# Weight splits queued before the last recurrence and its scans, and odd Fourier weights cast among the evictions of the even map

## The chip, the cores and the metric

The kernel runs on one core of a Trainium2 chip. The metric is the device time of one execution in microseconds (us), the median over runs. Lower is better.

## What is computed

One layer of a diffusion backbone for 512 latent tokens and 256 context tokens of width 1024, all in float32. The first half is a token mixer, the second a layer of sixteen experts.

```python
h = modulate(rmsnorm(x), shift, scale)              # latent and context alike
z = h @ w_in                                        # [Fourier | RG-LRU input | GeLU gate | gate A | gate B]
y_four = fourier_mix(z_F) @ w_four                  # real part of a 2-D DFT, 4 groups of 128 channels
u = dwconv(z_X); r = rglru_bidir(u)                 # gates, exp, linear scans in both directions
y_rnn = (gelu(z_G) * r) @ w_lru
x = x + g1 * ((sigmoid(z_A) * y_four + sigmoid(z_B) * y_rnn) @ w_out)
x = x + g2 * expert_choice_ffn(modulate(rmsnorm(x), ...))   # 16 experts: gate, up, down
out = rmsnorm(x)
```

## The kernel before, in words

Everything is written out by hand: each engine runs its instructions in the order of the Python code, and an instruction that waits holds up all that stands behind it on its engine.

**Weights and splits.** A product with float32 accuracy is made of three TensorE passes (`mm3`, L428 to L430): high part by high part, high by low, low by high. So each block of weights (1024 rows by 256 columns, `raw`, 1 MB) is split after it has landed: ScalarE casts the high part `wH` (L230), and VectorE subtracts it from the block to make the low part `wL` (L231), each in two halves. `split(j)` does this for block j, `use(j)` splits block j+1 and hands out block j, `SP.pop(j)` hands out block j alone. There are two buffers of `wH` and `wL`, so block j+2 is split into the buffers of block j, and its cast waits until TensorE has read block j for the last time. There are three buffers of `raw`. The list `seq` gives the order of the loads on SyncE's queue, and each split or accumulation that frees a buffer issues the next (`load_next`). The blocks of `w_ada` (for the modulation vectors) stand between them at places given by `ada_at`: VectorE accumulates such a block in nine instructions (`ada_acc`, L273 to L278), and TensorE reduces it over the partitions later (`ada_red`, L289 or L293).

**The Fourier stage** (some 55 to 95 us). For each of eight column blocks j TensorE computes the even part `ye` (weights `we`, the sum `wo` of two halves of `w_four`; L430, L642), and afterwards for each j the odd part `yo` (weights `wd4`, split from the difference `A4` by `split_four`, L609 and L610). `ye` is copied by ScalarE into a tile `y4[j]` (L643). There are four PSUM buffers for `ye` and `yo`. Behind each copy stands `modulate`, which prepares one block of the context (`cH` on ScalarE L422, GpSimd L423, `cL` on VectorE L426). The difference A4 - B4 is made by GpSimd in four instructions (L541), behind a chain of small ones for the recurrence (`lru_b`). The tiles `y4` lie in a pool that is opened where the pool `ad` was closed, and B4 had its place in that pool.

**The recurrence** (95 to 260 us). For each of eight heads h: `zX` (TensorE), convolution (VectorE), gates, `lru(h-1)` (ScalarE tanh, exp, sqrt; VectorE L701, L711; GpSimd L712) and `scans(h-2)` (VectorE L720 to L724, GpSimd L726, which adds the two directions into `yr`).

**The GeLU stage** (245 to 307 us). Blocks J_G to J_G+3 give `zG(0)` to `zG(3)`, 48 matmuls each, then follows `zB`. The loop over i writes out, for each engine, the products of block i, and behind them: for i = 0 `scans(6)` and `lru(7)`; for i = 1 `scans(7)`, the close of the recurrence's pools, the opening of the pool for `gH` and `gL`, and `g_evac(0)`; for i = 2 and 3 `g_evac(i - 1)`, and at last `g_evac(3)`. `g_evac(i)` does for two heads a GeLU on ScalarE (L791), the product with `yr` on VectorE (L792), the cast to `gH` (L793) and the subtraction to `gL` (L794). In i = 3 a tick after the fifth k of `zG(3)` calls `ada_red`.

**The rest.** Gate B and the map `w_lru` (`zB`, `yR`), the output projection, the router, and from about 465 us on the experts. Their 302 MB of weights are loaded through a ring of buffers (`eload`): the first loads are issued in the output projection, and each further one when TensorE has used a tile of the ring.

Of the kernel before, what the change touches and what calls it, by code (L numbers as in the profile page):

```python
# [12 lines left out]
AF = mybir.ActivationFunctionType  # L13
# [63 lines left out]
def layer(ctx: ExitStack, tc: tile.TileContext, I, out):  # L77
    nc = tc.nc
    pe, act, dve, pool = nc.tensor, nc.scalar, nc.vector, nc.gpsimd
# [78 lines left out]
    for i in range(4):  # L158
# [3 lines left out]
    J_X, J_G, J_B, J_O = 2, 10, 14, 22  # L162
# [1 line left out]
    ada_cols = ([1024 + 256 * i for i in range(4)] + [256 * i for i in range(4)] +  # L164
                [2048 + 256 * i for i in range(4)] + [4096 + 256 * i for i in range(4)] +
                [3072 + 256 * i for i in range(4)] + [5120 + 256 * i for i in range(4)])
    ada_at = {j: [p] for j, p in zip([J_X + 1, J_X + 3, J_X + 5, J_X + 7, J_G + 1] + list(range(J_G + 3, J_O + 2)), range(8, 24))}
    seq = [("a", 0), ("a", 4), ("f", 0), ("a", 1), ("f", 1), ("a", 5), ("f", 2), ("a", 2), ("a", 6), ("f", 3), ("a", 3), ("a", 7)]
    seq += [("4", 0), ("4", 1), ("w", 2)]
    for i in range(2, NW):  # L170
# [9 lines left out]
    def load_next():  # L180
        n = st["load"]
        if n >= len(seq):
            return
        st["load"] += 1
        kind, j = seq[n]
        if n in (3, 4, 8, 9, 13):
            t = ad.tile([P, 8, 256], F32, tag="ad", bufs=2, name=f"raw{n}")
        else:
            t = stage.tile([P, 8, 256], F32, tag="raw", bufs=AHEAD, name=f"raw{n}")
        if kind == "w":  # L190
            nc.sync.dma_start(t, W[j][0])
        elif kind == "f":
            t = f2(t)[:, 0:1024].rearrange("p (k e) -> p k e", k=2)
            nc.sync.dma_start(t, w_in[256 * j:256 * j + 256, 0:512].rearrange("(k p) e -> p k e", p=P))
        elif kind == "4":
            t = t.rearrange("p (a k) e -> p a (k e)", a=2)
            if j:
                nc.sync.dma_start(t, I["w4b"])
            else:
                for c in range(2):  # L200
                    nc.sync.dma_start(t[64 * c:64 * c + 64], flat(I["w_four"], P * c * D, [[D, 64], [256 * D, 2], [1, D]]))
        else:
            nc.sync.dma_start(t, w_ada[:, ada_cols[j]:ada_cols[j] + 256].rearrange("(p k) e -> p k e", k=KD))
        raws[kind, j] = t
        if n == 11:
            nc.sync.dma_start(dc, I["dft_c"])
            nc.sync.dma_start(xc, I["ctx"][0].rearrange("(n p) d -> p n d", p=P))
        if n == 13:
            nc.sync.dma_start(dt, I["dft_t"])
            for q in range(4):  # L210
                nc.sync.dma_start(w6[32 * q:32 * q + 4, :].rearrange("p (a e) -> p a e", a=2),
                                  flat(I["w_four"], 64 * D + P * q, [[P * D, 4], [512, 2], [1, P]]))
# [6 lines left out]
    SP = {}  # L219

    def split_half(j, h, copy=None):
        if j >= NW:
            return
        nk = W[j][1]
        if j not in SP:
            SP[j] = (take("w", j), stage.tile([P, nk, 256], F32R, tag="wH", bufs=2, name=f"wH{j}"),
                     stage.tile([P, nk, 256], F32R, tag="wL", bufs=2, name=f"wL{j}"))
        raw, wH, wL = SP[j]
        a = slice(h * nk // 2, (h + 1) * nk // 2)
        (copy or act.copy)(wH[:, a], raw[:, a])  # L230
        dve.tensor_sub(wL[:, a], raw[:, a], wH[:, a].bitcast(F32))  # L231
        if h:
            SP[j] = (wH, wL)
            load_next()

    def split(j, copy=None):
        for h in range(2):
            split_half(j, h, copy)
# [182 lines left out]
    def modulate(k, v, src, tmp, dH, dL, eng, late=()):  # L421
        act.activation(dH, src, AF.Identity, bias=modc[:, k, v:v + 1], scale=s1[:, k, v:v + 1])  # L422
        eng.tensor_scalar(tmp, src, s1[:, k, v:v + 1], modc[:, k, v:v + 1], op0=OP.mult, op1=OP.add)  # L423
        while late:
            late.pop()()
        dve.tensor_sub(dL, tmp, dH.bitcast(F32))  # L426
# [94 lines left out]
    A4, B4 = take("4", 0), take("4", 1)  # L521
# [29 lines left out]
    def use(j, copy=None):  # L551
        split(j + 1, copy)
        return SP.pop(j)
# [50 lines left out]
    def split_four(t, a, o):  # L604
        if not o:
            o.append(stage.tile([P, 2, D], F32R, tag="wH", bufs=2, name="w4H"))
            o.append(stage.tile([P, 2, D], F32R, tag="wL", bufs=2, name="w4L"))
        q = slice(512 * a, 512 * a + 512)
        act.copy(o[0][:, :, q], t[:, :, q])  # L609
        dve.tensor_sub(o[1][:, :, q], t[:, :, q], o[0][:, :, q].bitcast(F32))  # L610
# [3 lines left out]
    we, wd4 = [], []  # L614
# [8 lines left out]
    z = ct(0, "f6")  # L623
    cosines(z[:, 0:258], lambda b: P6[:, b].rearrange("p q c -> p (q c)"), E6.rearrange("p q c -> p (q c)"))
    put((8, 9), z[:, 0:258])
    for a in range(2):
        split_four(A4, a, wd4)
    load_next()

    def y4_mm(o, w, f, j, last):  # L630
        cc = slice(P * j, P * j + P)
# [4 lines left out]
    for j in range(KD):  # L636
        z = ct(1 + j, "ye")[:, 0:258]
        y4_mm(z, we, 0, j, False)
        q, c6 = 32 * (j % 4), P * (j // 4)
        r6 = slice(q, q + 32)  # L640
        for i, (a, b) in enumerate(((0, 8), (0, 9), (1, 8))):
            pe.matmul(z, w6s[r6, a, c6:c6 + P], fT[r6, b, 0:258], start=False, stop=i == 2, tile_position=(q, 0))  # L642
        act.copy(y4[j][:, 0:257], z[:, 0:257])  # L643
        modulate(j, 1, xcT[:, j, :], xcT[:, j, :], cH[:, j, :], cL[:, j, :], pool)
    split_half(J_X, 0)
    for j in range(KD):
        z = ct(1 + j, "yo")[:, 0:256]
# [12 lines left out]
    yr = bt.tile([P, H, T], F32, tag="bt", name="yr")  # L660
# [32 lines left out]
    def lru(h, mid=None):  # L693
        u = U.pop(h)
        r = {(d, i): GP.pop((h, d, i)) for d in range(2) for i in range(2)}
        tps = {}
        for d in range(2):
            q = 8 * d + h
            tps[d] = lr.tile([P, TA], F32, tag="tp", bufs=3, name=f"tp{h}")
            act.activation(tps[d], r[d, 0], AF.Tanh, bias=c2[:, q:q + 1], scale=c2[:, q:q + 1])  # L700
            dve.scalar_tensor_tensor(r[d, 1], r[d, 1], 1.0, u, op0=OP.add, op1=OP.mult)  # L701
        for d in range(2):
            q = 8 * d + h
            act.activation(r[d, 0], r[d, 0], AF.Exp, bias=c4n[:, q:q + 1], scale=c4n[:, q:q + 1])
        for d in range(2):
            act.activation(tps[d], tps[d], AF.Sqrt, scale=0.25)
        if mid:
            mid()
        for d in range(2):
            a, b, s = r[d, 0], r[d, 1], tps[d]  # L710
            dve.scalar_tensor_tensor(s, a, 1.0, s, op0=OP.add, op1=OP.mult)  # L711
            pool.tensor_tensor(b, s, b, op=OP.mult)  # L712
        LR[h] = r, tps

    def scans(h):
        r, tps = LR.pop(h)
        for d in range(2):
            a, b, s = r[d, 0], r[d, 1], tps[d]
            if d == 0:
                dve.tensor_tensor_scan(s, a, b, 0.0, OP.mult, OP.add)  # L720
            else:
                dve.tensor_tensor_scan(s[:, 0:TC][:, ::-1], a[:, 0:TC][:, ::-1], b[:, 0:TC][:, ::-1],
                                       0.0, OP.mult, OP.add)
                dve.tensor_tensor_scan(s[:, TC:TA][:, ::-1], a[:, TC:TA][:, ::-1], b[:, TC:TA][:, ::-1],  # L724
                                       s[:, 0:1], OP.mult, OP.add)
        pool.tensor_tensor(yr[:, h, :], tps[0][:, TC:TA], tps[1][:, TC:TA], op=OP.add)  # L726
# [57 lines left out]

    zG = {}

    def g_evac(i):
        z = zG.pop(i)
        for c in range(2):
            j = 2 * i + c  # L790
            act.activation(z[:, c, :], z[:, c, :], AF.Gelu_apprx_tanh)  # L791
            dve.tensor_mul(yr[:, j, :], z[:, c, :], yr[:, j, :])  # L792
            act.copy(gH[:, j, :], yr[:, j, :])  # L793
            dve.tensor_sub(gL[:, j, :], yr[:, j, :], gH[:, j, :].bitcast(F32))  # L794

# [9 lines left out]

    TICK = {0: g_tick, 3: ada_tick}
    for i in range(4):
        w = use(J_G + i) if i else SP.pop(J_G)
        zG[i] = (gt if i == 2 else zt)("zG")
        for c in range(2):  # L810
            zcols(w, zG[i][:, c, :], c, lambda k: TICK.get(i, lambda k: None)(KD * c + k))
        if i == 0:
            scans(H - 2)
            lru(H - 1)
            continue
        if i == 1:
            scans(H - 1)
            close_lr()
            close_hc()
            gp, close_gp = sb("gp", "right")  # L820
            gH = gp.tile([P, H, T], F32R, name="gH")
            gL = gp.tile([P, H, T], F32R, name="gL")
        g_evac(i - 1)
        if i == 1:
            ada_red()
            ada_acc(J_G + 1)
    g_evac(3)

    mH = []
# [2 lines left out]
    for i in range(4):  # L832
        w = use(J_B + 2 * i)
        th = sg.tile([P, 2, 512], F32, tag="th", bufs=2, name="thB")
        for c in range(2):
            z = ct(c, "zB")
# [123 lines left out]
    w = use(J_O)  # L960
# [420 lines left out]
```

## Time and profile before

| | |
|---|---|
| median of 3 runs | 1184.53 us (1184.46 to 1188.39) |
| the profiled execution's own time | 1183.71 us |
| its span, first to last instruction | 1181.9 us |
| busy in the span: TensorE, VectorE, ScalarE, GpSimd | 96%, 47%, 25%, 10% |
| mean granted TensorE clock | 0.989 |
| read from HBM | 364.43 MB |

The profile shows one execution, with times in us from the start of its span. The busy share is an average over stages with different limits: where an engine waits, and for whom, is read stage by stage. A granted clock of 1.00 is 2.4 GHz, 0.50 is 1.2 GHz.

### The profile page before, as it was taken

How to read it: one execution, taken by the hardware profiler on the slowest of the kernel's cores; microseconds unless marked ns; L12 is line 12 of the kernel's file. 1: busy time of each engine (PE TensorE's matmuls, PEld its weight loads, DVE VectorE, ACT ScalarE, POOL GpSimd, SP SyncE). 2: the span in 40 equal slices, each digit the busy share in tenths (PEclk: the TensorE clock that was granted, in tenths of full speed). 3: DMA queues.
4: the chain of work that ended last, by engine and by line, in shares of the span. 5: the costliest groups of instructions: out<-in, count | busy, mean ns of one | idle time of the engine just before them, and what ended most of it. 6: DMA issues, size and time to landing. Idle time of an engine off the chain costs nothing. (4 is left out here: it accounts for less than half of the span.)

```text
span 1181.9 us, 16740 instructions
## 1 busy us (share of the span) xinstructions
PE 1140.5 (96%) x6870; PEld 684.7 (58%) x6888; DVE 552.3 (47%) x1090; ACT 294.1 (25%) x457; POOL 115.0 (10%) x120
## 2 busy tenths in 40 slices
PE   8999999998999999999999999999999999999986
PEld 4778777776888897545445445454444345345333
DVE  5545898877767675233432332342332332332124
ACT  5452776764423222101001001001001001001004
POOL 4163333422000000000000000000000000000002
PEclk9989999998999999999999999999999999999998
DMA  8922321332544697889999999999999999999995
GB/s 303 320 88 92 125 80 54 116 107 67 194 167 150 206 367 318 311 348 416 367 424 424 424 423 424 423 424 423 424 423 424 425 423 424 423 425 424 424 413 217
DMA packets 115435, 368.01 MB, mean 311 GB/s; under 512 B 8912, under 2 KB 61656, under 8 KB 115232
## 3 DMA queue, kind: packets, MB, share of 16 engines
q1 hardware_dynamic: 112688, 363.52, 77.6%
q0 software_dynamic: 1088, 2.18, 0.6%
q10 hardware_dynamic: 1584, 1.25, 0.4%
q8 instruction: 54, 0.88, 0.3%
q14 instruction: 21, 0.17, 0.0%
HBM read 364.43 MB, written 2.10 MB: 310 GB/s over the span
## 5 line engine op out<-in xcount | busy, mean ns | idle before, releaser
L1152 PE MATMUL G<-ew,g 128*64 128x384 f32 x960 | 171.4, 493 | 2.6 <-DMA ew<-in_w_gate_e 2.1
L1152 PE MATMUL U<-ew,g 128*64 128x384 f32 x928 | 166.0, 493 | 6.8 <-DMA ew<-in_w_up_e 6.7
L1177 DVE TENSOR_TENSOR ac<-ac,sc 128x512 f32<-128x512 f32 x112 | 72.0, 684 | 97.5 <-PE sc L1171 97.5
L1152 PEld LDWEIGHTS G<-ew,g 128*64 128x64 f32 x960 | 62.9, 136 | 85.0 <-issue 64.0
L1152 PEld LDWEIGHTS U<-ew,g 128*64 128x64 f32 x928 | 60.7, 136 | 86.9 <-issue 59.8
L1288 POOL TENSOR_TENSOR o<-ac,ew 128x512 f32<-128x512 f32 (+1 forms) x8 | 7.8, 1000 | 880.7 <-ACT o L1284 880.7
L1254 DVE SCALAR_TENSOR_TENSOR wc<-Y,gc,g 128x512 f32<-128x512 f32 x15 | 11.3, 751 | 146.2 <-PE Y L1251 146.2
L1251 PE MATMUL Y<-ew,wa 128*64 128x512 f32 x312 | 74.1, 597 | 2.2 <-ACT wa L1240 2.2
L1251 PE MATMUL Y<-ew,wd 128*64 128x512 f32 x312 | 74.9, 594 | 0.0
L231 DVE TENSOR_TENSOR wL<-raw,wH 128x1024 fp32r<-128x1024 f32 x48 | 64.7, 1382 | 14.9 <-ACT wH L230 14.8
L1240 ACT COPY wa<-T 128x384 f32<-128x384 f32 x16 | 7.7, 479 | 250.3 <-PE T L1239 250.3
L1213 ACT ACTIVATE wc<-G 128x768 f32<-128x768 f32 x16 | 13.0, 811 | 180.5 <-PE G L1152 180.5
L230 ACT CAST wH<-raw 128x1024 fp32r<-128x1024 f32 x48 | 48.2, 1044 | 22.0 <-PE zO L430 18.5
L1124 PEld LDWEIGHTS xg<-wa,x 128*128 128x128 f32 x448 | 51.1, 192 | 0.2
L1124 PE MATMUL xg<-wa,x 128*128 128x128 f32 x448 | 51.2, 275 | 0.0
L1251 PEld LDWEIGHTS Y<-ew,wd 128*64 128x64 f32 x312 | 23.5, 137 | 47.3 <-issue 39.6
L1090 DVE TENSOR_SCALAR wc<-wa,score 128x128 bf16<-128x128 f32 (+3 forms) x63 | 24.0, 380 | 56.3 <-ACT wa L1083 56.3
L1257 ACT CAST wb<-wc 128x512 fp32r<-128x512 f32 x15 | 9.3, 618 | 153.8 <-DVE wc L1254 153.8
L1251 PEld LDWEIGHTS Y<-ew,wa 128*64 128x64 f32 x312 | 21.4, 136 | 43.7 <-issue 35.4
L712 POOL TENSOR_TENSOR th<-tp,th 128x768 f32<-128x768 f32 x16 | 38.5, 2426 | 63.1 <-DVE tp L711 63.1
L1171 PEld LDWEIGHTS sc<-wb 64*128 64x128 f32 x240 | 23.6, 184 | 35.9 <-issue 35.9
L688 ACT ACTIVATE th<-ga,lru_c 128x768 f32<-128x768 f32 x32 | 28.9, 905 | 41.8 <-PE ga L686 41.8
(361 smaller groups left out, 2181.5 us busy)
## 6 DMA issues: line engine op xcount, KB each, us to landing
ew<-in_w_gate_e SPq DMA_DIRECT2D x120, 768.0 KB, 14.7
ew<-in_w_up_e SPq DMA_DIRECT2D x116, 768.0 KB, 14.7
ew<-in_w_down_e SPq DMA_DIRECT2D x111, 768.0 KB, 14.7
raw<-in_w_ada SPq DMA_DIRECT2D x24, 1024.0 KB, 5.5
raw<-in_w_in SPq DMA_DIRECT2D x16, 1024.0 KB, 5.1
wd<-in_w_down_e SPq DMA_DIRECT2D x8, 768.0 KB, 12.0
we<-in_w_down_e SPq DMA_DIRECT2D x8, 768.0 KB, 14.8
raw<-in_w_lru SPq DMA_DIRECT2D x4, 1024.0 KB
```

What stands on the lines that cost most here:

```text
L230: (copy or act.copy)(wH[:, a], raw[:, a])
L231: dve.tensor_sub(wL[:, a], raw[:, a], wH[:, a].bitcast(F32))
L688: act.activation(t, gf[:, 256:1024], AF.Tanh, bias=(hbi if i else hba)[:, 8 * d + h:8 * d + h + 1], scale=0.5)
L712: pool.tensor_tensor(b, s, b, op=OP.mult)
L1090: dve.tensor_scalar(GT[c][:, 0:m], sB[:, 0:m], s, None, op0=OP.is_lt)
L1124: pe.matmul(a[k // 4][:, P * (k % 4) + q.start:P * (k % 4) + q.stop], x[:, n, P * k:P * k + P], oh[:, n, q], start=n == 0, stop=n == NT - 1)
L1152: pe.matmul(t[64 * f:64 * f + 64, n, 0:384], xg[:, k, c:c + CAP], w[:, o:o + 384], start=k == 0, stop=k == KD - 1, tile_position=(0, 64 * f))
L1171: pe.matmul(a[dh][:, c], w, v, start=j == 0, stop=j == 1, tile_position=(64 * dh, 0))
L1177: dve.tensor_add(xs, xs if e else x[:, n, q], a[dh])
L1213: act.activation(v3(sl), G[:, :, 0:384], AF.Silu)
L1251: pe.matmul(yp[64 * dh:64 * dh + 64, :], hT[j // 3][:, j % 3, 64 * f:64 * f + 64], w[:, 512 * i:512 * i + 512], start=f == 0 and j == 0, s ...
L1254: dve.scalar_tensor_tensor(y, yp, gc[:, e % 3:e % 3 + 1], g2, op0=OP.mult, op1=OP.mult)
```

## The change

Three things are moved, nothing is added or left out in the computation.

1. In the Fourier stage the two halves of `split_four(A4, ...)` no longer stand ahead of the copies of `ye`, but behind the copy and the `modulate` of j = 4 and of j = 6. The load behind them moves to the end of that loop.
2. In the GeLU stage the split of J_G+2 stands between `scans(6)` and `lru(7)`, and the split of J_G+3 ahead of `scans(7)`. Blocks J_G+1 and J_G+2 are therefore handed out without a further split. Before, J_G+2 was split behind `lru(7)`, and J_G+3 behind `g_evac(0)` and an accumulation.
3. The GeLU and the product of heads 0 and 1 (`g_mul`) stand ahead of the split of J_G+3; `g_evac(0)` has only the cast and the subtraction left. The block of `w_ada` that was loaded ahead of J_G+3 is now loaded behind it (`ada_at`), and still accumulated at the end of i = 1.

```diff
-    ada_at = {j: [p] for j, p in zip([J_X + 1, J_X + 3, J_X + 5, J_X + 7, J_G + 1] + list(range(J_G + 3, J_O + 2)), range(8, 24))}
+    ada_at = {j: [p] for j, p in zip([J_X + 1, J_X + 3, J_X + 5, J_X + 7, J_G + 2] + list(range(J_G + 3, J_O + 2)), range(8, 24))}
...
     put((8, 9), z[:, 0:258])
-    for a in range(2):
-        split_four(A4, a, wd4)
-    load_next()
...
         act.copy(y4[j][:, 0:257], z[:, 0:257])
         modulate(j, 1, xcT[:, j, :], xcT[:, j, :], cH[:, j, :], cL[:, j, :], pool)
+        if j in (4, 6):
+            split_four(A4, j // 2 - 2, wd4)
+    load_next()
     split_half(J_X, 0)
...
+    def g_mul(i, c):
+        j = 2 * i + c
+        z = zG[i]
+        act.activation(z[:, c, :], z[:, c, :], AF.Gelu_apprx_tanh)
+        dve.tensor_mul(yr[:, j, :], z[:, c, :], yr[:, j, :])
+
     def g_evac(i):
-        z = zG.pop(i)
         for c in range(2):
             j = 2 * i + c
-            act.activation(z[:, c, :], z[:, c, :], AF.Gelu_apprx_tanh)
-            dve.tensor_mul(yr[:, j, :], z[:, c, :], yr[:, j, :])
+            if i:
+                g_mul(i, c)
             act.copy(gH[:, j, :], yr[:, j, :])
...
     for i in range(4):
-        w = use(J_G + i) if i else SP.pop(J_G)
+        w = use(J_G + i) if i > 2 else SP.pop(J_G + i)
...
         if i == 0:
             scans(H - 2)
+            split(J_G + 2)
             lru(H - 1)
             continue
         if i == 1:
+            for c in range(2):
+                g_mul(0, c)
+            split(J_G + 3)
             scans(H - 1)
...
         if i == 1:
             ada_red()
-            ada_acc(J_G + 1)
+            ada_acc(J_G + 2)
```

On ScalarE in the Fourier stage (`w4H` is the high part of the odd weights, `y_0` to `y_7` the tiles `y4`; in brackets the engines whose semaphores an instruction waits for), before:

```order
L579 CAST fT<-f_718 128x258 [waits PE_49]
L609 CAST w4H<-raw_420 128x2x512 [waits DMAHW5_49,Pool_49]
L609 CAST w4H<-raw_420 128x2x512 [waits Pool_49]
L643 COPY y_0_622<-ye 128x257 [waits DMAHW7_49,PE_49]
L422 ACTIVATE cH<-zs,modc,s_82 128x256 [waits Activation_49]
L643 COPY y_1_623<-ye 128x257 [waits PE_49]
```

and with the change:

```order
L579 CAST fT<-f_718 128x258 [waits PE_49]
L640 COPY y_0_622<-ye 128x257 [waits DMAHW7_49,PE_49,Pool_49]
L422 ACTIVATE cH<-zs,modc,s_82 128x256 [waits Activation_49]
L640 COPY y_1_623<-ye 128x257 [waits PE_49]
L422 ACTIVATE cH<-zs,modc,s_82 128x256
L640 COPY y_2_624<-ye 128x257 [waits PE_49]
L422 ACTIVATE cH<-zs,modc,s_82 128x256
L640 COPY y_3_625<-ye 128x257 [waits PE_49]
L422 ACTIVATE cH<-zs,modc,s_82 128x256
L640 COPY y_4_626<-ye 128x257 [waits PE_49]
L422 ACTIVATE cH<-zs,modc,s_82 128x256 [waits Activation_49]
L609 CAST w4H<-raw_420 128x2x512 [waits DMAHW5_49]
```

The casts have moved behind the fifth and the seventh copy, and the wait for GpSimd has moved with the place, not with the casts: it now stands at the first copy.

On VectorE in the GeLU stage (`wL` low parts of weights, `tp` and `th` tiles of the recurrence of head 7; L720 to L724 are its scans), before:

```order
L701 SCALAR_TENSOR_TENSOR th_7_2079<-th_7_2079,u_1956 128x768
L711 SCALAR_TENSOR_TENSOR tp_2107<-th_7_2055,tp_2107 128x768
L711 SCALAR_TENSOR_TENSOR tp_2110<-th_7_2071,tp_2110 128x768
L231 TENSOR_TENSOR wL_2122<-raw_1970,wH_2121 128x1024 x2
L720 SCALAR_TENSOR_TENSOR tp_2107<-th_7_2055,th_7_2063 128x768
L722 SCALAR_TENSOR_TENSOR tp_2110<-th_7_2071,th_7_2079 128x256
L724 SCALAR_TENSOR_TENSOR tp_2110<-th_7_2071,tp_2110,th_7_2079 128x512
L792 TENSOR_TENSOR yr<-zG,yr 128x512
L794 TENSOR_TENSOR gL<-yr,gH 128x512
L792 TENSOR_TENSOR yr<-zG,yr 128x512
L794 TENSOR_TENSOR gL<-yr,gH 128x512
L295 TENSOR_TENSOR g_94<-adb_2197,g_94 128x256
```

and with the change:

```order
L231 TENSOR_TENSOR wL_2108<-raw_1970,wH_2107 128x1024 x2
L701 SCALAR_TENSOR_TENSOR th_7_2063<-th_7_2063,u_1956 128x768
L701 SCALAR_TENSOR_TENSOR th_7_2079<-th_7_2079,u_1956 128x768
L711 SCALAR_TENSOR_TENSOR tp_2115<-th_7_2055,tp_2115 128x768
L711 SCALAR_TENSOR_TENSOR tp_2118<-th_7_2071,tp_2118 128x768
L791 TENSOR_TENSOR yr<-zG,yr 128x512 x2
L231 TENSOR_TENSOR wL_2183<-raw_2017,wH_2182 128x1024 x2
L720 SCALAR_TENSOR_TENSOR tp_2115<-th_7_2055,th_7_2063 128x768
L722 SCALAR_TENSOR_TENSOR tp_2118<-th_7_2071,th_7_2079 128x256
L724 SCALAR_TENSOR_TENSOR tp_2118<-th_7_2071,tp_2118,th_7_2079 128x512
L799 TENSOR_TENSOR gL<-yr,gH 128x512 x2
L295 TENSOR_TENSOR g_94<-adb_2205,g_94 128x256
```

The low part of J_G+2 now stands ahead of head 7's recurrence, and that of J_G+3, with two products ahead of it, where that of J_G+2 stood. Behind L295 and L296 the nine instructions of the accumulation follow in both; before, the low part of J_G+3 came only after them.

## Rows read from the trace of the kernel before

**Rows 1.** Windows: us; busy (count) PE, PEld, DVE, ACT, POOL; PEclk, DMA share, GB/s.

```profile
270.00:300.00 30.00, 24.63 (x89) 19.11 (x88) 24.05 (x30) 14.70 (x19) 6.47 (x3) 0.83 0.32 106
600.00:800.00 200.00, 199.08 (x1355) 98.98 (x1356) 70.09 (x164) 16.86 (x31) 0.00 (x0) 1.00 1.02 424
```

**Rows 2.** Waits of SyncE's queue, 395 to 520 us: total us, times, longest.

```profile
SPq L901 <- PE G L1152: 23.3, 8, 6.9
```

**Rows 3.** TensorE's timeline, 273 to 308 us: start, us, instruction, [idle before <-releaser].

```profile
273.50 0.59 PE L293 MATMUL adb<-acc,one_eps 128*128 128x256 f32 x2
...
276.70 0.50 PE L430 MATMUL zG<-hH,wL 128*128 128x512 f32 x1 [2.15 <-DVE wL L231]
...
281.61 0.40 PE L430 MATMUL zG<-hL,wH 128*128 128x512 f32 x1
...
292.93 0.79 PE L430 MATMUL zG<-hH,wL 128*128 128x512 f32 x1 [3.22 <-DVE wL L231]
...
299.32 0.40 PE L430 MATMUL zG<-hL,wH 128*128 128x512 f32 x1
...
306.79 0.40 PE L430 MATMUL zB<-hH,wH 128*128 128x512 f32 x1
```

**Rows 4.** Windows of 2 us (columns as in rows 1).

```profile
80.00:82.00 2.00, 2.00 (x9) 1.68 (x8) 1.21 (x3) 2.00 (x6) 2.00 (x3) 0.54 0.59 191
278.00:280.00 2.00, 2.00 (x7) 1.52 (x6) 2.00 (x2) 0.00 (x0) 0.34 (x1) 0.53 0.00 0
```

**Rows 5.** Timeline of the Fourier stage, 71 to 95 us, GpSimd, TensorE and ScalarE.

```profile
71.25 5.97 POOL L541 TENSOR_TENSOR raw<-raw,raw 128x512 f32<-128x512 f32 x4
...
73.99 0.62 PE L642 MATMUL ye<-fT,w6s 32*128 32x258 f32 x3
...
75.46 0.63 PE L642 MATMUL ye<-fT,w6s 32*128 32x258 f32 x3
77.26 1.04 ACT L609 CAST w4H<-raw 128x1024 fp32r<-128x1024 f32 x1 [2.41 <-POOL raw L541]
78.21 0.37 ACT L643 COPY y<-ye 128x257 f32<-128x257 f32 x1
...
78.63 0.51 PE L430 MATMUL ye<-fT,w4H 128*128 128x258 f32 x2 [2.54 <-ACT y L643]
...
93.83 0.28 PE L430 MATMUL yo<-fT,w4L 128*128 128x256 f32 x1
...
94.53 0.28 PE L430 MATMUL yo<-fT,w4L 128*128 128x256 f32 x1
94.65 0.40 PE L762 MATMUL zX<-hH,wH 128*128 128x512 f32 x1
```

**Rows 6.** Timeline of VectorE, 244 to 316 us.

```profile
263.69 1.28 DVE L724 TENSOR_TENSOR_SCAN tp<-th,tp,th 128x512 f32<-128x512 f32 x1
...
273.80 5.63 DVE L231 TENSOR_TENSOR wL<-raw,wH 128x1024 fp32r<-128x1024 f32 x2
279.35 1.74 DVE L720 TENSOR_TENSOR_SCAN tp<-th,th 128x768 f32<-128x768 f32 x1
...
291.32 0.42 DVE L278 TENSOR_TENSOR acc<-acc,acc 128x256 f32<-128x256 f32 x1
291.66 2.35 DVE L231 TENSOR_TENSOR wL<-raw,wH 128x1024 fp32r<-128x1024 f32 x2
```

**Rows 7.** Timeline of GpSimd, 244 to 316 us.

```profile
273.16 5.18 POOL L712 TENSOR_TENSOR th<-tp,th 128x768 f32<-128x768 f32 x2 [6.19 <-DVE tp L711]
```

**Rows 8.** Timeline of ScalarE, 244 to 316 us.

```profile
267.00 1.03 ACT L700 ACTIVATE tp<-th,lru_c 128x768 f32<-128x768 f32 x1 [5.92 <-POOL yr L726]
...
274.65 1.28 ACT L791 ACT_TABLE_LOAD   x1
...
284.40 0.62 ACT L793 CAST gH<-yr 128x512 fp32r<-128x512 f32 x1 [7.87 <-POOL yr L726]
```

**Rows 9.** Waits of TensorE, 0 to 520 us: total us, times, longest.

```profile
PE xt L390 <- DVE zs L386: 4.1, 2, 3.4
```

## The prediction, made before the change was run

> **What bounds the kernel now.** I read the windows by stage first. In the expert stage TensorE is busy for 199.08 of 200 us, and the transfers run at 424 GB/s [rows 1]: both are near their limit, and the change touches nothing there. The stretch from 270 to 300 us is another matter: TensorE is busy for 24.63 of 30 us, at a mean granted clock of 0.83 [rows 1]. What is saved there, or in the Fourier stage, reaches the end if the experts start earlier by as much. The waits of SyncE's queue speak for it: between 395 and 520 us the loads of expert weights wait 23.3 us for TensorE to give tiles of the ring back [rows 2], so the stream of weights follows TensorE. I pass a saving on one to one.
>
> Then I read TensorE's own timeline in the two places. In the GeLU stage it stops for 2.15 us ahead of 276.70 and for 3.22 us ahead of 292.93, both times for the low part of a weight block on VectorE [rows 3]. In the Fourier stage it stops for 2.54 us ahead of 78.63, for ScalarE to copy a `ye` out of PSUM [rows 5]. Then the granted clock falls to its lower level, seen as a mean of 0.54 from 80 to 82 us and of 0.53 from 278 to 280 [rows 4]; behind 292.93 the pace of the matmuls shows it.
>
> The second price is as large as the first. At the full clock 32 matmuls take 7.47 us (299.32 to 306.79), 0.233 each [rows 3]. From 276.70 to 281.61 stand 14 matmuls, 3.27 us at that pace, in 4.91: the fall cost 1.6. From 292.93 to 299.32 stand 14 and a reduction of 0.36, 3.63 us, in 6.39: it cost 2.8 [rows 3]. In the Fourier stage a `ye` takes 1.47 us at the full clock (73.99 to 75.46) and a `yo` 0.70 (93.83 to 94.53); four and eight of them make 11.5 us, but 78.63 to 94.65 is 16.0 [rows 5]: the fall cost 4.5.
>
> **The Fourier stage, part by part.** The two casts leave the place ahead of the copies. The second had started at 77.26, when GpSimd's four subtractions were done (71.25 + 5.97 = 77.22), and the first copy followed at 78.21 [rows 5]. With the casts gone one would think that the copies start when `ye` is there, at 76. They do not: `y4` lies where B4 lay, GpSimd's subtractions read B4, and in the order of the changed kernel the first copy itself waits for GpSimd. So it starts at 77.27, and 0.94 us is saved; TensorE resumes at 77.7 and its stall is 1.6 us instead of 2.54.
>
> What follows depends on the clock. If it holds, four `ye` and eight `yo` take 11.5 us from 77.7, to 89.2. A copy (0.37 [rows 5]) and its context block keep ScalarE for some 0.8 us, and each block's share on GpSimd is as long, so by my estimate the first odd cast, behind the fifth pair, comes at about 81, and its low part on VectorE, behind the fifth context block, ends at about 84; the first `yo`, at 83.6 (77.7 + 4 x 1.47), needs that for its third pass, and waits some 0.3 us. The second half is ready at 86.1, half a microsecond before the fifth `yo` asks for it. So `zX` starts at 89.5 instead of 94.65: 5.1 us. If the clock falls again at 80, only the first copy's 0.94 and the greater part of one more `ye` at the full clock (0.7) are saved: 1.6 us. The bounds are 0.9 and 5.1.
>
> The rows do not tell which. Stalls of 2.15 us and more were followed by a fall, a stall of 3.4 us near the start [rows 9] by none; none of 1.6 us is to be found. I take the fall as slightly the likelier, since the rest of `ye` stands behind this stall as it did behind the old one, and there the clock stayed low through all of it. What the later load, and `cL` behind two subtractions on VectorE, cost is nothing: both are ready microseconds before `zX`.
>
> **The GeLU stage, part by part.** The buffers of J_G+2 are free when `zG(0)` ends, 48 matmuls (11.2 us) ahead of 273.50, that is at 262.3. ScalarE's two casts take 2 us; VectorE is free from its scans at 265.0 [rows 6] and needs 2.4 us, up to twice that beside GpSimd. Both are done by 270, and `zG(2)` starts at 273.75 with all its weights. Head 7's chain is not pushed, since its second step on ScalarE waits for GpSimd's sum behind those scans, 5.92 us, to 267.00 [rows 8]. The 2.15 us and the fall behind them (1.6) go.
>
> Next is J_G+3. VectorE is free at 273.80, as before [rows 6], and ScalarE from its sqrt by then. The GeLU table (1.28 us [rows 8]), two GeLUs and two products in turn, each 0.6 to 0.7 us like the cast of 512 columns (0.62 [rows 8]), end at 276.7. The two subtractions took 5.63 us beside GpSimd's multiplications, which run to 278.34 [rows 6, 7], and 2.35 alone [rows 6]; they would start at 277.0, when 1.3 of those 5.2 us are left, and I take 3.1, to 280.1. So J_G+3 is ready 5 us before `zG(3)` wants it at 285.0, and the 3.22 us and their fall of 2.8 go too. Together 9.8 us are removed.
>
> But **a new wait** takes their place. The scans of head 7 move from 279.35 [rows 6] to 280.1, and with them the cast that ends the wait for GpSimd, from 284.40 [rows 8] to 285.15. Behind it the accumulation of the `w_ada` block ended at 291.74 [rows 6], 7.3 us later; two products of 0.7 have left this piece, so it now ends at 291.1. TensorE needs this block for the reduction after the fifteenth matmul of `zG(3)`. It came there just ahead of 299.32 [rows 3] before, long after; now it comes at 273.75 + 63 x 0.233 = 288.5, and waits 2.5 us. Behind it stand all the rest of `zG(3)` and `zB`. With the subtractions at their undisturbed 2.35 us the wait is 1.8; with the whole 5.63, 5.1.
>
> The wait of 2.5 us is nearest to the one of 2.15, so I add that one's fall, 1.6 (bounds 0 and 2.8). `zB` then starts at 288.5 + 2.5 + 0.36 + 33 x 0.233 + 1.6 = 300.7 instead of 306.79 [rows 3]: **6.1 us saved**. With no fall it would be 6.8, not 7.7, because VectorE's backlog, three microseconds closer to TensorE than before, then makes the next reduction in `zB` wait some 0.9 for a PSUM buffer. At the dear end (5.1 and 2.8) 2.3 are left.
>
> The moved load costs nothing: the place of J_G+3 in SyncE's queue is now the earlier one, 20 us before its cast.
>
> **The sum.** 1.6 and 6.1 make 7.7 us: 1183.71 - 7.7 = 1176.0 for an execution like the profiled one. That one lies 0.8 below the median of 1184.53, so I say 1177.
>
> **A rule beside it.** The rows show falls of the clock after stalls of 2.15 and 2.54 us [rows 3 to 5]. The Trainium skill, page "TensorE: Matmul & The Clock Gate", section "Why this matters for your kernels", warns only of idle gaps longer than either. By that rule neither of the two stalls that are left would cost the clock, and the sum would be that of the second rival below; the falls above speak against it.
>
> **The rivals.**
> - *The clock holds in the Fourier stage* (its stall is only 1.6 us), and falls after the new wait: 5.1 + 6.1 = 11.2, to 1173.3. For it: no fall in these rows follows a stall so short. Against it: the same work followed the stall of 2.54 us.
> - *It holds in both places*: 5.1 + 6.8 = 11.9, to 1172.6. Against it: the fall after 2.15 us.
> - *VectorE is disturbed as before* beside GpSimd: the wait at the reduction is 5.1 us with a fall of 2.8, and the Fourier stage gives 0.9: 3.2 in all, to 1181.3. Against it: the subtractions now start 3.2 us later, when GpSimd is nearly done.
> - *The gain is swallowed by the experts*, because their transfers set the end by themselves: 1184. Against it: the loads wait for TensorE [rows 2].
> - *Slower*: ScalarE stands at the cast of J_G+2 until `zG(0)` ends, with head 7's tanh behind it; if that and the subtractions ahead of L701 push head 7's whole chain, its scans, the pool behind them and the accumulation slide, and TensorE waits at the reduction of `zG(3)`. This decides when the wait there passes 8 us (288.5 + 8.1 + 0.36 + 7.7 + 2.8 = 307.5, the old start of `zB` and most of the Fourier stage's 0.9); at 14 us the kernel is at 1190. Against it: ScalarE's idle 5.92 us there [rows 8] holds the casts' 2 us.
>
> **How the numbers follow.** My forecast (fall in the Fourier stage, new wait with a fall) has 0.42, with its own range of 1174.5 to 1180; the clock holding in the Fourier stage 0.34, in both 0.05, the disturbed VectorE 0.10, the swallowed gain 0.05, slower 0.04. The range 1171.5 to 1181.5 takes in the first three with their bounds and most of the fourth. A measurement of this kernel can tell about 0.5% from no change, 5.9 us: faster means below 1178.6. That is four fifths of the forecast (0.34) and the two cases where the clock holds (0.39): 0.73. Within 0.5% are the rest of the forecast, the disturbed VectorE and the swallowed gain: 0.23. Slower: 0.04.
>
> **What would show it.** In the changed profile the first copy of a `ye` should start within 0.1 us of GpSimd's last subtraction, near 77.3, and TensorE's stall there be 1.6 us; the granted clock from 80 to 88 us decides between the first two cases, and `zX` starts near 93 or near 89.5. `zG(2)` and the weights of `zG(3)` should show no wait for `wL`; instead TensorE waits for VectorE's accumulation at the reduction (L289), 2 to 3 us. I am wrong if the copies start at 76, if that reduction does not wait, or if `zB` starts less than 4 us earlier against `zX` than before.

## The result, and the profile after

The changed kernel takes **1173.57 us** (median of 5 runs, 1172.96 to 1183.9) where the kernel before takes 1185.26 in the same session: a ratio of 0.9916, with a 95% interval of 0.9889 to 0.9943. By the ratio that is 10 us faster. The forecast was 1177.0, its range 1171.5 to 1181.5. Two of the five runs took 1180.03 and 1183.9 us, at a mean granted clock of 0.991 and 0.986 where the other three had 0.994 to 0.996. Each kernel has one profile, so a stall or a fall of the clock that is read below is that of one execution. The profiled execution took 1173.57 us with a span of 1171.7, against a span of 1181.9 before.

The windows of the two stages of [rows 1], with the stretches of [rows 4], and two more behind the stalls. The columns are PE, PEld, DVE, ACT and POOL busy, then the granted clock, the DMA share and GB/s:

```profile
79.00:90.00 11.00, 11.00 (x80) 9.77 (x79) 7.37 (x13) 10.83 (x25) 7.23 (x8) 1.00 0.12 35
80.00:82.00 2.00, 2.00 (x14) 1.62 (x13) 1.06 (x3) 2.00 (x6) 1.94 (x3) 1.00 0.04 8
270.00:300.00 30.00, 27.90 (x115) 22.16 (x114) 23.49 (x40) 10.79 (x17) 5.27 (x3) 0.94 0.38 128
278.00:280.00 2.00, 2.00 (x10) 1.61 (x9) 1.73 (x2) 0.00 (x0) 0.15 (x1) 1.00 1.02 335
288.00:291.00 3.00, 3.00 (x9) 2.32 (x8) 1.89 (x3) 2.13 (x4) 0.00 (x0) 0.51 0.95 329
600.00:800.00 200.00, 199.18 (x1348) 99.42 (x1346) 67.13 (x160) 18.75 (x36) 0.00 (x0) 1.00 1.02 424
```

The expert stage is as it was (199.18 of 200 us, 424 GB/s). In the GeLU stage TensorE is busy for 27.90 of 30 us instead of 24.63, at a mean clock of 0.94 instead of 0.83. From 79 to 90 us the clock is at its upper level throughout, where [rows 4] had 0.54. One stretch of low clock is left, from 288 to 291 us.

The Fourier stage in the timeline, to be laid beside [rows 5]:

```profile
71.80 0.50 PE L430 MATMUL ye<-fT,w4H 128*128 128x258 f32 x2
...
73.18 4.99 POOL L541 TENSOR_TENSOR raw<-raw,raw 128x512 f32<-128x512 f32 x4
...
78.20 0.38 ACT L640 COPY y<-ye 128x257 f32<-128x257 f32 x1 [5.92 <-POOL raw L541]
78.63 0.51 PE L430 MATMUL ye<-fT,w4H 128*128 128x258 f32 x2 [0.91 <-ACT y L640]
...
82.00 1.05 ACT L609 CAST w4H<-raw 128x1024 fp32r<-128x1024 f32 x1
84.47 1.07 ACT L609 CAST w4H<-raw 128x1024 fp32r<-128x1024 f32 x1
84.51 0.50 PE L430 MATMUL yo<-fT,w4H 128*128 128x256 f32 x2
90.53 0.39 PE L762 MATMUL zX<-hH,wH 128*128 128x512 f32 x1
```

The first copy starts at 78.20, right behind GpSimd's last subtraction (73.18 + 4.99 = 78.17). The stall of 2.54 us is one of 0.91, and no fall of the clock follows. From the first `ye` to `zX` it now takes 18.73 us (71.80 to 90.53), against 24.50 before (70.15 to 94.65): **5.8 us**.

The GeLU stage, to be laid beside [rows 3, 6]:

```profile
269.80 0.59 PE L293 MATMUL adb<-acc,one_eps 128*128 128x256 f32 x2
...
273.55 2.65 DVE L231 TENSOR_TENSOR wL<-raw,wH 128x1024 fp32r<-128x1024 f32 x2 [0.27 <-ACT wH L230]
...
286.71 0.42 DVE L278 TENSOR_TENSOR acc<-acc,acc 128x256 f32<-128x256 f32 x1
...
287.19 0.60 PE L289 MATMUL adb<-one_eps,acc 128*128 128x1 f32 x4 [2.10 <-DVE acc L278]
287.66 0.48 PE L430 MATMUL zG<-hH,wH 128*128 128x512 f32 x1
...
288.75 0.63 PE L430 MATMUL zG<-hH,wH 128*128 128x512 f32 x1
...
291.61 0.39 PE L430 MATMUL zG<-hL,wH 128*128 128x512 f32 x1
...
296.97 0.40 PE L430 MATMUL zB<-hH,wH 128*128 128x512 f32 x1
```

Neither `zG(2)` nor `zG(3)` waits for a weight block any more. In the place of these waits TensorE stands for 2.10 us at the reduction L289, until VectorE has accumulated the `w_ada` block. Behind it ten matmuls take 3.95 us (287.66 to 291.61) where 2.33 are due: the fall cost 1.6. From the reduction L293 to `zB` it takes 27.17 us, against 33.29 in [rows 3]: **6.1 us**.

The two make 11.9, and `zB` starts 9.8 us earlier (296.97 against 306.79). Of the difference 0.4 us are given back by the change itself, between `zX` and L293 (179.27 us against 178.85), where the first `zA` now waits for VectorE. This row is from the waits by engine (us in total, times, longest):

```profile
PE zA L430 <- DVE wL L231: 0.3, 1, 0.3
```

The other 1.65 us are not the change's: the first `ye` started that much later than in the execution before, and no instruction up to there has been moved. In the nine kernels that are alike up to that point it comes anywhere from 70.15 to 74.23 us. In this execution VectorE's first sum of the even weights waited for a load of the start-up, for which it did not wait in the execution before:

```profile
58.79 1.23 DVE L530 TENSOR_TENSOR wo<-raw,raw 128x1024 f32<-128x1024 f32 x1 [1.49 <-DMA raw<-in_w_in]
```

### The profile page after: what moved, and what is told of

Its sections match the earlier page's. It is cut to its first block, busy times and chain, and to the rows that moved or that the text cites. A ratio compares the mean times of both kernels' runs of the same rounds, so it can differ in the third digit from the quotient of the medians.

```text
span 1171.7 us, 16760 instructions
## 1 busy us (share of the span) xinstructions
PE 1134.9 (97%) x6888; PEld 678.5 (58%) x6888; DVE 548.8 (47%) x1090; ACT 293.4 (25%) x457; POOL 115.3 (10%) x120
## 6 DMA issues: line engine op xcount, KB each, us to landing
wd<-in_w_down_e SPq DMA_DIRECT2D x8, 768.0 KB, 11.9
```

## The experiments

The theory after the result: each part of the change is worth its stage's 6 us by itself, and the Fourier stage gave more than forecast because its stall became too short for a fall of the clock. What made it so short was to be found out. The measure in what follows is a distance within one profile, from the first `ye` to `zX` and from L293 to `zB`; where a program starts its Fourier stage varied by several us from profile to profile. Ratios are to the kernel before, in the same session.

**The Fourier part alone.** The kernel before with these lines of the change:

```diff
-    for a in range(2):
-        split_four(A4, a, wd4)
-    load_next()
...
+        if j in (4, 6):
+            split_four(A4, j // 2 - 2, wd4)
+    load_next()
```

> The kernel before with the Fourier part of the change alone. My theory: the two parts add up, and the Fourier part is worth what the profile after shows from the first `ye` to `zX`, 24.50 us before against 18.73 after, so 5 to 6 us: 1179 to 1180 against 1185, with no fall of the clock behind the stall and a stall of 0.6 to 1.0 us. Rival 1 (the likeliest case of the prediction): the clock held in the profile after by luck, and falls here: 1.6 us gained, 1183.5. Rival 2: what is saved here is lost again at the waits of the GeLU stage, which are not removed in this kernel: 0 to 1 us, 1184 to 1185.

Measured: ratio 0.9963 (0.9946 to 0.9981). From `ye` to `zX` 18.70 us, with a stall of 0.86 and no fall. The GeLU stage keeps its two waits for `wL` (2.14 and 3.24 us) and takes 32.22 us. That is 1.1 us less than before with the same waits, all of it behind the second: from its end to `zB` it takes 12.82 us (288.51 to 301.33) where it took 13.86 (292.93 to 306.79), so the fall of the clock there cost less. In the stage the theory holds, and neither rival does. The ratio makes 4.4 us of the whole time (2.3 to 6.4), where 5 to 6 had been expected.

**The GeLU part alone.** The kernel before with the change's new `g_mul` and the earlier splits, and the Fourier lines as before (the lines against the changed kernel):

```diff
+    for a in range(2):
+        split_four(A4, a, wd4)
+    load_next()
...
-        if j in (4, 6):
-            split_four(A4, j // 2 - 2, wd4)
-    load_next()
```

> The kernel before with the GeLU part of the change alone. My theory: 6.1 us from the start of the second reduction of this stage to `zB` (33.29 before, 27.17 after), so 1179 against 1185, with the Fourier stage as before (stall near 2.5 us, clock at its lower level behind it) and the new wait of 2 us at the reduction in `zG(3)`. Rival 1: without the new fall behind that wait, 7.7 us, 1177.5. Rival 2: the new wait depends on what the Fourier part does to VectorE's backlog, and without it is gone, with its fall: 9.8 us, 1175.

Measured: ratio 0.9956 (0.9939 to 0.9972). From L293 to `zB` 27.17 us, as in the whole change to the hundredth, with a wait of 2.10 at the reduction. The Fourier stage has its stall of 2.83 us, the fall, and 26.12 us. The theory holds, and neither rival does. The gains of the two parts (0.37% and 0.44% of the time) add up to that of the whole change (0.84%) within their intervals, so nothing shows that one part needs the other.

**GpSimd first.** The changed kernel with GpSimd's subtractions ahead of its chain of small coefficients:

```diff
-    lru_b()
     for i in range(4):
         q = slice(256 * i, 256 * i + 256)
         pool.tensor_tensor(A4[:, :, q], A4[:, :, q], B4[:, :, q], op=OP.subtract)
+    lru_b()
```

> The changed kernel with GpSimd's four subtractions of the odd Fourier weights put ahead of its chain of small recurrence coefficients. My theory: the first copy of a `ye` waits for those subtractions and for nothing else, so here it starts as soon as `ye` is there, TensorE's stall of 0.91 us is gone, and the time falls by 0.9 us to 1172.5; executions in which the stall ends in a fall of the clock (4.5 us) would go too, which would make the spread of the runs smaller. Rival 1: the subtractions now run beside VectorE's sums and low parts of the even weights, slow them, and the first `ye` starts 1 us or more later: no change or slower, 1173.5 to 1175. Rival 2: something else holds the copies: same stall.

Measured: ratio 0.9907 (0.9889 to 0.9925), so no gain over the change that can be told. The stall at `ye` is gone, and from `ye` to `zX` it takes 17.48 us. But the first rival came true as well. Timeline and a window of this kernel:

```profile
60.40 0.42 DVE L498 TENSOR_TENSOR zs<-zs 128x256 f32<-128x256 f32 x1
60.73 1.52 DVE L499 TENSOR_TENSOR zs<-zs 128x256 f32<-128x256 f32 x1
62.17 1.48 DVE L498 TENSOR_TENSOR zs<-zs 128x256 f32<-128x256 f32 x1
...
60.70 2.67 POOL L540 TENSOR_TENSOR raw<-raw,raw 128x512 f32<-128x512 f32 x2 [8.29 <-DMA raw<-in_w_in]
...
67.64 1.86 PE L584 MATMUL fc<-dt,PC 128*128 128x258 f32 x4 [1.59 <-ACT zs L602]
```

```profile
68.00:72.00 4.00, 4.00 (x9) 2.35 (x8) 2.73 (x6) 3.37 (x7) 3.49 (x8) 0.50 0.06 15
```

Beside GpSimd's first two subtractions VectorE's small sums take 1.5 us instead of 0.42. TensorE then waits 1.59 us ahead of `fc`, a step of the Fourier transform ahead of `ye`, instead of 0.96 in the changed kernel, and now the clock falls there, to 0.50 from 68 to 72 us. A stall was traded for another one with a fall.

**GpSimd second.** The same four subtractions behind the first step of the chain, which waits for those sums:

```diff
     def lru_b():
         pool.tensor_tensor(zz, ax, zz, op=OP.mult)
+        for i in range(4):
+            q = slice(256 * i, 256 * i + 256)
+            pool.tensor_tensor(A4[:, :, q], A4[:, :, q], B4[:, :, q], op=OP.subtract)
...
     lru_b()
-    for i in range(4):
-        q = slice(256 * i, 256 * i + 256)
-        pool.tensor_tensor(A4[:, :, q], A4[:, :, q], B4[:, :, q], op=OP.subtract)
```

> The changed kernel with GpSimd's four subtractions behind the first step of its coefficient chain, which waits for VectorE's sums of the folds: so they no longer run beside those sums, which the last experiment slowed from 0.42 to 1.5 us. My theory: `fc` waits 1.0 us for ScalarE as in the profile after and not 1.6, no fall of the clock in the Fourier stage, the first copy starts when `ye` is there, and from the first `ye` to `zX` it takes 17.5 us (as in the last experiment) against 18.73: 1172.3 or 1.2 us under the changed kernel. Rival: GpSimd, wherever it stands, delays something on VectorE that TensorE waits for (the low parts of the even weights, 2.38 us), and the first `ye` starts 1 us later: no change.

Measured: ratio 0.9899 (0.9873 to 0.9925), median 1173.75. No stall at `ye`, no wait at `fc` in the list of waits (1.0 us had been expected), no fall, and 17.67 us from `ye` to `zX`: 1.1 less than in the change. The median, 0.2 us above that of the change, does not show it; the four runs lie between 1172.16 and 1179.1.

**The late reduction.** The changed kernel with the reduction in `zG(3)` behind the tenth contraction block:

```diff
     def ada_tick(k):
-        if k == 4:
+        if k == 9:
```

> The changed kernel with the reduction in `zG(3)` and the accumulation behind it 15 matmuls later (behind the tenth contraction block, not the fifth). My theory: the wait of 2.1 us for VectorE's accumulation and the fall of the clock behind it (1.6 us) are both gone: 3.7 us, 1170. Rival 1: VectorE's backlog is then the bound, and what is saved turns into a wait for the low part of the first `zB` block or at the next reduction: 1 to 2 us, 1172. Rival 2: the clock falls there for another reason than the wait: 2.1 us, 1171.5.

Measured: ratio 0.9902 (0.9874 to 0.993). From L293 to `zB` it takes 23.26 us instead of 27.17: 3.9 us, wait and fall together. Part of it comes back behind `zB`, where VectorE is the next to be late:

```profile
289.19 0.50 PE L289 MATMUL adb<-one_eps,acc 128*128 128x1 f32 x4
...
300.53 0.50 PE L430 MATMUL zB<-hH,wH 128*128 128x512 f32 x1 [0.41 <-DVE yr L791]
307.35 0.50 PE L430 MATMUL yR<-gH,wL 128*128 128x512 f32 x1 [0.47 <-DVE wL L231]
```

So the theory holds up to `zB`. Then VectorE's backlog takes back 0.9 us, as the first rival had it, though at other waits and a little less than the 1 to 2 us that it had named. The whole time shows no gain: the median is 1173.56, where the theory had 1170, and in the profile the last stretch of the program is 2.4 us longer than in the change (see the last section).

**A longer stall.** Two kernels, each the changed one with GpSimd work added behind L541, on which the first copy must wait too. One is a whole quarter, the other half of one:

```diff
+    pool.tensor_tensor(B4[:, :, 0:256], A4[:, :, 0:256], B4[:, :, 0:256], op=OP.subtract)
```

> The changed kernel with a fifth subtraction on GpSimd (1.25 us by 4.99 for four; its result goes to a buffer that is dead by then), which the first copy of a `ye` then waits for too: TensorE's stall becomes 2.2 us and nothing else changes. My theory: the length of this stall decides whether the clock falls behind it. After 2.2 us it falls, and `ye` to `zX` takes 18.73 + 1.25 + 3 to 4.5 = 23 to 24.5 us; median 1178. Rival: the cast and the subtraction that stood beside the stall in the kernel before made the difference; the clock holds, 20.0 us from `ye` to `zX`; median 1175.

```diff
+    pool.tensor_tensor(B4[:, :, 0:128], A4[:, :, 0:128], B4[:, :, 0:128], op=OP.subtract)
```

> The changed kernel with half a subtraction more on GpSimd (0.63 us): a stall of 1.5 us, the one that the prediction had worked out. My theory: the prediction took the wrong side for this length; the clock holds, and `ye` to `zX` takes 19.4 us; median 1174. Rival: the clock falls behind 1.5 us, as the prediction had it: 22.5 to 24 us, median 1177.5; then the only error was the length of the stall.

Measured: a stall of 1.82 us with the quarter and of 1.29 with half of it. The clock fell behind both; from `ye` to `zX` 25.22 and 24.72 us; ratios 0.9931 (0.9911 to 0.9952) and 0.9939 (0.9918 to 0.996). The rows and a window of the second:

```profile
77.87 0.72 POOL L542 TENSOR_TENSOR raw<-raw,raw 128x256 f32<-128x256 f32 x1
...
79.05 0.51 PE L430 MATMUL ye<-fT,w4H 128*128 128x258 f32 x2 [1.29 <-ACT y L641]
```

```profile
82.00:90.00 8.00, 8.00 (x31) 6.76 (x31) 4.65 (x8) 5.84 (x12) 3.80 (x5) 0.50 0.01 1
```

For the first of the two the theory holds in kind: the clock falls, though the stall is shorter than the 2.2 us expected and the 25.22 us are more than the 23 to 24.5. For the second it is wrong, and its rival is right about the fall: 0.38 us more of a stall than in the change cost 6.0 us in the stage, 5.6 of them for the fall. So the prediction's judgement, that a stall of 1.6 us would be followed by a fall, is borne out; the stall was not 1.6.

Both stalls came out shorter than expected because GpSimd began 1.09 us behind the first `ye` in these two profiles and 1.38 in that of the change. And the fall is dearer than the 4.5 us of the kernel before, because the clock stayed low for longer. Before, it rises again early in this window:

```profile
90.00:92.00 2.00, 2.00 (x17) 2.00 (x17) 1.83 (x4) 0.75 (x2) 0.65 (x1) 0.90 0.00 0
```

In the kernel with half of a quarter more it is still 0.50 from 90 to 94 us. From windows of 1 us the low stretch is, by estimate, 10.2 us long before and 13.7 in each of these two.

**Who makes GpSimd fast.** What had left GpSimd's neighbourhood with the change were ScalarE's casts and VectorE's low parts. One kernel puts both back for the first half of the weights, the other the cast alone (`"high"` does the cast, `"low"` the subtraction of `split_four`):

```diff
+    split_four(A4, 0, wd4)
...
-        if j in (4, 6):
+        if j == 6:
```

> The changed kernel with the cast and the low part of the first half of the odd weights back ahead of the `ye` loop, as before the change; the second half stays behind the seventh pair. My theory: it is VectorE's low part (1.23 us) beside GpSimd's four subtractions that makes these take 5.97 us instead of 4.99. So here they take 5.97 again, TensorE's stall is 1.6 to 1.9 us, the clock falls behind it, and from the first `ye` to `zX` it takes 24 to 25.5 us against 18.73; median near 1179. Rival 1: GpSimd's time has nothing to do with the low part; 4.99 us, a stall of 0.9, 18.7 us, median 1174. Rival 2: 5.97 us and a stall of 1.6 to 1.9, but the clock holds: 19.7 us, median 1175.

```diff
...
+    split_four(A4, 0, wd4, "high")
...
-            split_four(A4, j // 2 - 2, wd4)
+            split_four(A4, j // 2 - 2, wd4, "low" if j == 4 else None)
```

> The changed kernel with ScalarE's cast of the first half alone back ahead of the `ye` loop, and its low part on VectorE left behind the fifth pair. My theory: ScalarE's reading does not disturb GpSimd: four subtractions in 4.99 us, a stall of 0.9, the clock holds, 18.4 to 18.8 us from `ye` to `zX`; median 1173.5. Rival: it is ScalarE's cast that slows GpSimd (or both share in it): 5.5 to 6 us, a stall of 1.4 to 1.9 with a fall, 24 to 25.5 us; median 1179.

The kernel with both:

```profile
72.97 5.98 POOL L541 TENSOR_TENSOR raw<-raw,raw 128x512 f32<-128x512 f32 x4
75.53 1.05 ACT L609 CAST w4H<-raw 128x1024 fp32r<-128x1024 f32 x1 [3.45 <-POOL raw L541]
76.61 1.23 DVE L610 TENSOR_TENSOR w4L<-raw,w4H 128x1024 fp32r<-128x1024 f32 x1 [4.07 <-ACT w4H L609]
79.41 0.74 PE L430 MATMUL ye<-fT,w4H 128*128 128x258 f32 x2 [1.90 <-ACT y L641]
```

The kernel with the cast alone:

```profile
71.93 4.98 POOL L541 TENSOR_TENSOR raw<-raw,raw 128x512 f32<-128x512 f32 x4
74.47 1.05 ACT L610 CAST w4H<-raw 128x1024 fp32r<-128x1024 f32 x1 [3.44 <-POOL raw L541]
77.37 0.51 PE L430 MATMUL ye<-fT,w4H 128*128 128x258 f32 x2 [0.91 <-ACT y L643]
```

Measured: with the low part beside them the four subtractions take 5.98 us, the stall is 1.90, the clock falls, and it takes 25.30 us to `zX` (ratio 0.9912, 0.989 to 0.9934). With the cast alone they take 4.98, the stall is 0.91, no fall, 18.54 us (ratio 0.9885, 0.9861 to 0.9909). One subtraction of 1.23 us on VectorE thus holds GpSimd up by 1.0 us and is itself no longer than elsewhere (1.22 us in the change); ScalarE's cast holds GpSimd up by nothing. The theory holds in both. The Trainium skill, page "SBUF — State Buffer", section "Who interferes with whom", says that a VectorE instruction with two SBUF inputs contends with a GpSimd instruction that reads SBUF, that the order of issue decides who is blocked, and that ScalarE waits on nobody. The traces agree: 5.98 against 4.98, and which engine pays changes with the place (two of VectorE's sums paid 1.1 us each in the kernel with GpSimd first).

**Both stalls away.** The changed kernel with GpSimd second and the late reduction:

> The changed kernel with GpSimd's subtractions behind the first step of the chain, and the reduction of `zG(3)` 15 matmuls later: both stalls that the change left are gone. My theory: 1.2 us in the Fourier stage and 3.0 in the GeLU stage (3.9 from the first reduction to `zB`, of which two later waits give back 0.9, as measured with the late reduction alone): 4.2 us under the changed kernel, 1169.5. Rival: the experts' transfers, which TensorE waited 2.6 us longer for in the run with the late reduction, take it back: 1171.5 to 1172.5.

Measured: ratio **0.9889** (0.9858 to 0.9919), median 1171.66 us, 1169.25 at best, with 17.68 us from `ye` to `zX` and 23.26 from L293 to `zB`. What TensorE still waits for between 50 and 320 us:

```profile
PE ga L685 <- ACT th L688: 0.6, 1, 0.6
PE yR L430 <- DVE wL L231: 0.5, 1, 0.5
PE zB L430 <- DVE yr L791: 0.4, 1, 0.4
```

It alone is short in both stages, and its profiled time, 1169.79, is 3.8 us under that of the change, near the theory's 4.2. Its median lies where the rival had it, 1171.5 to 1172.5, though the last stretch of the profile is only 0.7 us longer than in the change. The runs cannot decide between the two: the medians differ by less than their spread. That this kernel beats the kernel before is shown; that it beats the change is shown in the two stages only.

All profiles together, in us, one execution of each kernel (L293 to `zB` depends on the GeLU part, the rest on the Fourier part; "half of one more" is the kernel with half of a quarter more):

| kernel | stall at `ye` | clock falls behind it | `ye` to `zX` | L293 to `zB` |
|---|---|---|---|---|
| before | 2.54 | yes | 24.50 | 33.29 |
| GeLU part alone | 2.83 | yes | 26.12 | 27.17 |
| low part early | 1.90 | yes | 25.30 | 27.19 |
| a quarter more | 1.82 | yes | 25.22 | 27.16 |
| half of one more | 1.29 | yes | 24.72 | 25.62 |
| changed | 0.91 | no | 18.73 | 27.17 |
| cast early | 0.91 | no | 18.54 | 25.63 |
| late reduction | 0.88 | no | 18.70 | 23.26 |
| Fourier part alone | 0.86 | no | 18.70 | 32.22 |
| GpSimd second | none | no | 17.67 | 27.17 |
| GpSimd first | none | no (at `fc`: yes) | 17.48 | 27.14 |
| both stalls away | none | no | 17.68 | 23.26 |

## Why the prediction was right, and where it was not

*The direction and the range* were right: faster by more than 0.5%, 1173.57 within 1171.5 to 1181.5. The likeliest case was not the one that came: it was the first rival, the clock holding in the Fourier stage and falling behind the new wait, whose 1173.3 us is 0.3 from the median measured. That closeness is in part luck: the rival had 11.2 us off the profiled execution, and 10.1 came off it. The Fourier stage gave 0.6 us more and the last stretch 0.3, but the late start took 1.65 and the wait at `zA` 0.4.

*The copies wait for GpSimd* (first copy within 0.1 us of its last subtraction): right, 0.03 us.

*The stall of 1.6 us* is **the step that failed**. It was the old stall less the 0.94 us between 77.27 and the old first copy, and it kept GpSimd's 5.97 us of [rows 5] as they were. But the change takes VectorE's low part away from beside GpSimd, and without it they are 4.99: 0.98 less, of which 0.28 was lost because GpSimd began 1.38 us behind the first `ye` and not 1.10, a distance that takes either size from profile to profile. That makes 0.9. The runs with the low part early and the cast early show it apart: 5.98 us and a stall of 1.90 with the low part, 4.98 and 0.91 without. The prediction had used the same contention in the other direction, for VectorE's subtractions beside GpSimd in the GeLU stage, and did not turn it round.

*The fall behind it*, and with it a gain of 1.6 us instead of 5.1: wrong as forecast, because the stall was shorter. At this place four profiles with stalls of 0.86 to 0.91 us have no fall and five with 1.29 to 2.83 have one, so a stall of 1.6 would have been on the dear side. That a short stall is never followed by a fall is not shown: the runs of the change that took 1180 us and more have no profile. The forecast's 1.6 us of gain would have been too high even with its fall (24.7 us at 1.29, against 24.50 before), because it took the price of a fall from the one execution of [rows 5].

*The odd casts between the evictions*: they began at 82.00 and 84.47, where the prediction, with its earlier start of `ye`, had 81 for the first. The stretch behind the stall took 11.9 us (78.63 to 90.53), and 11.8 had been worked out for it. So the 0.6 us by which the measured 5.8 is above the rival's 5.1 are the shorter stall.

*The GeLU stage*: right term by term. 6.1 us was forecast, and 6.1 measured from L293 to `zB`. The two waits for `wL` went, ScalarE's idle 5.92 us ahead of head 7's second step [rows 8] took the casts (2.08 us of it are left), J_G+3's low part took 2.65 us where 3.1 were taken, the new wait was 2.10 where 2.5 were, and its fall cost the 1.6 that had been carried over from the fall behind 2.15 us. Whether that fall comes is another matter: of eight profiles with this wait, two have none. In those two 7.7 us are saved, and no wait in `zB` follows, so the 0.9 us that the rival *it holds in both places* had put there is not borne out.

*A saving passes to the end one to one*: right for this pair of profiles. From the last matmul of the output projection (`zO`) to the end of the span it takes 727.2 us before and 726.9 after. Over all the profiles that stretch varies by 4 us (see the last section), which can hide a saving of that size. SyncE's loads of expert weights still wait for TensorE, for 30.7 us between 395 and 520 us, where [rows 2] had 23.3:

```profile
SPq L910 <- PE G L1161: 30.7, 13, 7.4
```

*The rule that the prediction had set beside the sum*, from the page "TensorE: Matmul & The Clock Gate" of the Trainium skill, section "Why this matters for your kernels", gave the right outcome for the Fourier stage, but the runs do not bear it out: it warns only of gaps longer than these stalls, and the clock fell behind one of 1.29 us at `ye` and behind the 2.10 us at the reduction.

## What to carry to other kernels

When work leaves an engine's neighbourhood, price again what ran beside it: a VectorE subtraction of 1.23 us with both operands in SBUF, the on-chip memory, held GpSimd's subtractions up by 1.0 us here, and the gain of the Fourier part hung on parting them (25.30 us with the low part back, 24.50 before, 18.73 in the change). Where a stall ends in a fall of TensorE's clock, its length is worth much less than the fall (0.4 us of stall, 5.6 of fall here), so work the length out to a tenth, from durations as they will be and not as they were. And judge such changes by distances inside a stage of the profile: where the code of a stage was the same and the clock did the same, they agreed to 0.1 us, while whole times of one kernel were 3 to 11 us apart.

## What the runs showed of the hardware that was not expected

At one place the fall of the clock follows the length of the stall, but not everywhere. Eight profiles have the wait of 2.1 us at the reduction L289. In six of them L293 to `zB` takes 27.1 to 27.2 us; in two, with the same wait, it takes 25.6, and the clock held. The window behind the wait in one of the two, the kernel with the cast early:

```profile
286.00:290.00 4.00, 4.00 (x20) 3.28 (x20) 2.37 (x5) 2.89 (x5) 0.00 (x0) 1.00 0.78 262
```

The changed kernel shows 0.51 from 288 to 291 us. What the two have in common that the six have not, the profiles do not say; it stays open, and so does how much of the spread between the runs of one kernel it makes. Nor is the longest stall of the kernel before followed by a fall: near its start TensorE stands for 3.36 us, and 0.9 us after it goes on two matmuls of 512 columns take 0.60 us together, where a single one took 0.63 in the low stretch of the change (288.75 above):

```profile
13.34 1.07 PE L390 MATMUL xt<-cst,zs 128*128 128x128 f32 x8 [3.36 <-DVE zs L386]
14.24 0.60 PE L310 MATMUL xt<-onesb 128*128 128x512 bf16 x2
```

The last stretch varies on its own. From the last `zO` to the end it takes 726.4 to 727.6 us in eight of the twelve profiles and 729.3 to 730.7 in the other four, in which the nine last loads of the down projection are issued over 23.3 to 23.5 us instead of 22.2 to 22.4. How early the experts start does not decide it: the kernel with both stalls away, the earliest, has 727.6 and GpSimd second, 0.1 us later, 730.2, while the one with half of a quarter more, 8 us later, has 730.7. What does decide it stays open.
